# Values of the forgetting attention in one wide projection, and the memory's value columns moved one head pair earlier

## The chip, the cores and the metric

The kernel runs on one core of a Trainium2 chip. The core has a matrix engine (TensorE, PE in the rows; its weight loads are listed apart as PEld), a vector engine (VectorE, DVE), an activation engine (ScalarE, ACT), a general engine (GpSimd, POOL) and a queue that issues transfers (SyncE, SP). They run side by side, each through its own list of instructions in order, and wait for each other through semaphores. The metric is the time of one execution on the device in microseconds (us); the median of the runs counts.

## The reference

One layer of a hybrid encoder, 512 frames, width 1024. Cut to what matters here:

```python
hn = rmsnorm(h, norm_mix_g)
fq, fk, fv, ff, gq, gf, gi, gg = split(hn @ w_in)        # fq, fk, fv: 8 heads of 64
fox_out = fox_attention(fq, fk, fv, log_sigmoid(ff + b)) # causal, blocks of 128 queries
rec = hgrn2_chunkwise(gq, gf, gi, lbs) ...               # gated linear recurrence, 4 heads of 128
h = h + concat(fox_out, rec) @ w_out
mem_n = rmsnorm(mem, norm_mem_g)                         # 256 memory rows
k, v = split(mem_n @ w_xkv)                              # 1024 columns each
h = h + softmax((rmsnorm(h) @ w_xq) k / 16) v @ w_xo     # 4 heads of 256
h = h + square(relu(rmsnorm(h) @ w1)) @ w2
return rmsnorm(h, final_norm_g)
```

All inputs and results are float32, and every large product is made of three matmuls of a split type: each operand is kept as a rounded part (hi) and a remainder (lo), and hi*hi, hi*lo and lo*hi are added up.

## The kernel before

**Weights.** A list (`specs`, from line 126) names the weight panels in the order of their use. `next_panel` (line 214) keeps the panels loaded one ahead: a panel arrives as two units of 128x1024 elements, each of which ACT rounds to the hi part (`wh...`, line 171) and DVE subtracts to get the lo part (`wl...`, line 175). There are four buffers for hi and four for lo, so a unit can be split only when the PE has read the unit four places earlier. In the names, wh10b is the second unit of panel 10.

**Two ways to project.** `proj_tm` takes a panel of 256 columns: for every block of 128 frames, and every one of 8 slices of the width, three matmuls of 256 columns (lines 249 to 251). `proj_wide` and `gemm_wide` take 512 columns as two panels of four slices each: matmuls of 512 columns (lines 264 to 266) into four PSUM banks at once.

**Fill.** The order of the PE's instructions is that of the code (the other engines are ordered by a scheduler). The serial parts, the recurrence over four chunks and then the forgetting attention, are interleaved with a queue of independent projections: `fill.run(us)` takes steps from the queue until their nominal time reaches a credit, and `fill.until(name)` takes them until the projection of that name is done.

**Forgetting attention.** Four pairs of heads, for each four query blocks and two heads: 32 units. Per unit, in this order: the bias (POOL, `bi`), the scores (PE, `ps`, two matmuls with the keys `kh` and `kl`), a `fill.run(2.2)`, the product with the values of the unit three places before (PE, `pv`), and the transpose of the previous unit's probabilities (PE, `pt`). Between scores and transpose DVE takes the maximum (line 936), ACT the exponential (line 938), DVE normalises (line 940), and the transposed tile is copied out of PSUM (`pts`). A pair's queries and keys come from `fox_proj(p)` in the queue: 24 matmuls for the queries (`pq`) and 24 for the keys (`pk`); then DVE scales the keys (`ks`, line 759), ACT writes the rounded keys in four pieces (`kh`, lines 762 and 763, two pieces for each head) and DVE the remainders (`kl`, line 764). Before the first unit of pair p the code calls `fill.until("proj"+p)`.

**What the queue holds.** The values (`fv`) are projected in two panels of 256 columns: the first (for pairs 0 and 1) ahead of unit 2, the second in the steps of pair 1, finished by `fill.until("fv256")` before pair 2. The memory's rows are transposed (`mnt`) between the steps of `fox_proj(1)`; then follow the memory's value columns, 0 to 255 (`xv0`) in pair 0, the middle 512 (`xvw`) and the last 256 (`xv3`) in pair 2, and its four key panels (`xk`). What is left in the queue after the last unit is run before the next projection (`wo`).

Of the kernel before, what the change touches and what calls it, by code (L numbers as in the profile page):

```python
# [12 lines left out]
AF = mybir.ActivationFunctionType  # L13
# [4 lines left out]
S = 512  # L18
NT = S // P
# [3 lines left out]
WT = 256  # L23
FH = 8
FD = 64
# [6 lines left out]
GF = 5  # L32
WARM, WARM2 = 7, 4
P1, P2, P3, P4, PW = 20, 20, 20, 10, -20
MT, NF, V0, LAG = 3, 2, 1, 3
F1, F2, F3, F4, B1 = 1.6, 2.7, 1.5, 1.0, 2.0
A1, A2 = 1.4, 0.8
X1, X2, X3, X4 = 1.5, 2.0, 1.5, 2.0
# [4 lines left out]
def emit(  # L43
# [24 lines left out]
    x, mem, w_in, w_out = x[0], mem[0], w_in[0], w_out[0]  # L68
# [24 lines left out]
    def s4(shape, name, dt=F32):  # L93
        return s4p.tile([P] + shape, dt, tag="s4", name=name)
# [18 lines left out]
    def mm(name, shape=(S,)):  # L113
        return mmp.tile([P] + list(shape), F32, tag="mm", name=name)

    def pvt(name):
        return pvp.tile([P, S], F32, tag="pv", name=name)
# [11 lines left out]
    def panel(w, n0):  # L129
        return [(slice(0, WT), w[:, n0 : n0 + WT].rearrange("(k p) n -> p k n", p=P))]  # L130

    def wide(w, n0):

        return [[(slice(0, S), w[k0 * P : (k0 + 4) * P, n0 : n0 + S].rearrange("(k p) n -> p k n", p=P))] for k0 in (0, 4)]

    specs = []
# [4 lines left out]
    def pair(p):  # L141
        return [
            (slice(0, P), w_in[:, p * P : (p + 1) * P].rearrange("(k p) n -> p k n", p=P)),
            (slice(P, 2 * P), w_in[:, 512 + p * P : 512 + (p + 1) * P].rearrange("(k p) n -> p k n", p=P)),
        ]

    xv = [panel(w_xkv, D), *wide(w_xkv, D + WT), panel(w_xkv, D + 3 * WT)]
    specs += [pair(0), panel(w_in, 1024), pair(1), *xv[0:V0], pair(2), panel(w_in, 1024 + WT), pair(3), *xv[V0:]]
    for j in range(4):
        specs.append(panel(w_xkv, j * WT))  # L150
    for w in (w_out, w_xq, w_xo):
# [60 lines left out]
    def next_panel():  # L212
        while len(stream) < min(state["used"] + 2, len(specs)):
            for split in load_next():
                with ahead(PW):
                    split()
        r = stream[state["used"]]
        state["used"] += 1
        return r
# [95 lines left out]
    fill = Fill()  # L315
# [140 lines left out]
    with tc.manual_schedule(engines={mybir.EngineType.Activation, mybir.EngineType.DVE}):  # L456
# [94 lines left out]
        def qt_(h):  # L551
            return (Mv, Sa)[h % 2][h // 2][:, h % 2, :]
# [27 lines left out]
    for hp in range(2):  # L580
        wt = next_panel()
        for j in range(2):
            h = 2 * hp + j
# [6 lines left out]
    def proj_tm(dst, n0, func, name):  # L590
        wt = next_panel()
        for tp in range(2):
            ps = mm(f"{name}{n0}{tp}", (2, WT))
            for j in range(2):
                yield from gemm_tm(ps[:, j, :], wt, hn_hi, hn_lo, 2 * tp + j)
            for j in range(2):
                tb = 2 * tp + j
                ac.activation(dst(tb, n0), ps[:, j, :], func, scale=r0[:, tb : tb + 1])
# [4 lines left out]
    def proj_wide(dst, func, name):  # L603
        pss = [mm(f"{name}{tb}") for tb in range(NT - 1)] + [pvt(f"{name}3")]

        def done(tb, ps):
            ac.activation(dst[tb // 2][:, tb % 2, :], ps, func, scale=r0[:, tb : tb + 1])

        yield from gemm_wide(pss, hn_hi, hn_lo, done)
# [3 lines left out]
    fvt = []  # L613
# [25 lines left out]
    for hp in range(2):  # L639
# [8 lines left out]
        for j in range(2):  # L648
            h = 2 * hp + j
# [38 lines left out]
    for li, m in enumerate(mlev):  # L688
# [21 lines left out]
        for hp, ps in enumerate(lvs):  # L710
# [18 lines left out]
            for j in range(2):  # L729
                h = 2 * hp + j  # L730
                qv, kv, fv = halves(qt_(h), m), halves(kt_(h), m), halves(F_[:, j, :], m)
# [3 lines left out]
            fv = halves(F_.rearrange("p h t -> p (h t)"), m)  # L735
# [39 lines left out]
        fill.run(F4)  # L775


    def new_fv():
        t = s4([NT, WT], f"fv{len(fvt)}")
        fvt.append(t)  # L780
        return lambda tb, n0: t[:, tb, :]

    fill.add(proj_tm(new_fv(), 0, AF.Identity, "fv"), "fv0")
    fF = {}

    def fox_rows(p):
# [6 lines left out]
    def load_mem(t):  # L793
        m_ = s4([D], f"mt{t}")
        gp.dma_start(m_, mem[t * P : (t + 1) * P, :])
        norm_rows(m_, f"m{t}")
        mt.append(m_)

    load_mem(0)


    mx_hi, mx_lo = act_tile("mx_hi"), act_tile("mx_lo")
# [21 lines left out]
    for c in range(NT):  # L824
        cs = slice(c * P, (c + 1) * P)
        it = iv[c // 2][:, c % 2, :].rearrange("p (h v) -> p h v", v=P)
        gt = gg[c // 2][:, c % 2, :].rearrange("p (h v) -> p h v", v=P)
        po = sc(f"po{c}", (4, P))
        for h in range(4):
            te.matmul(po[:, h, :], Ag[h // 2][:, (h % 2) * 4 + c, :], it[:, h, :], start=True, stop=c == 0)  # L830
            if c > 0:
                te.matmul(po[:, h, :], qt_(h)[:, cs], St[:, h, :], start=False, stop=True)
        if c < NT - 1:
            pst = sc(f"pst{c}", (4, P))
            for h in range(4):
                te.matmul(pst[:, h, :], kts[c][:, h, :], it[:, h, :], start=True, stop=True)
            if c < NT - 2:
                k_T(c + 1)
            with ahead(P2):
                Sn = t2(f"S{c}", F32, (4, P))  # L840
                if c == 0:
                    ve.tensor_copy(Sn, pst)
                else:
                    for h in range(4):
                        ve.scalar_tensor_tensor(
                            Sn[:, h, :], St[:, h, :], Fg[h // 2][:, h % 2, c * P : c * P + 1], pst[:, h, :], op0=ALU.mult, op1=ALU.add
                        )
                St = Sn
        with ahead(P1):
            hs = sm(4, f"hs{c}")  # L850
            for h in range(4):
                j = t2(f"hj{c}{h}", F32, (P,))
                ac.activation(j, po[:, h, :], AF.Square, scale=128.0 ** -0.5, accum_out=hs[:, h : h + 1])
            hr = rstd_of(hs, 4, f"hr{c}")
            rec = t2(f"rec{c}", F32, (4, P))
            for h in range(4):
                ve.scalar_tensor_tensor(rec[:, h, :], po[:, h, :], hr[:, h : h + 1], gt[:, h, :], op0=ALU.mult, op1=ALU.mult)
        fill.run(H1)
        if c == MT:
            load_mem(1)  # L860
        if c == NF:
            fox_rows(0)
        if pending is not None:
            to_mix(*pending)
        pending = (c, rec)
        fill.run(H2)
# [11 lines left out]
    def mem_v_wide():  # L878
        js = slice(WT, 3 * WT)

        def done(t, ps):
            ac.activation(xvh[t][:, js], ps, AF.Copy)
            ve.tensor_tensor(xvl[t][:, js], ps, f(xvh[t][:, js]), ALU.subtract)

        yield from gemm_wide([mm(f"xvw{t}") for t in range(2)], me_hi, me_lo, done)
# [70 lines left out]
    def fox_out(p, tb):  # L956
        if tb == 0:
            fpv[p] = pvt(f"pv{p}")
        pv = fpv[p]
        ts_ = slice(tb * P, (tb + 1) * P)  # L960
        for sb in range(tb + 1):
            for j in range(2):
                h = 2 * p + j
                te.matmul(
                    pv[64 * j : 64 * j + 64, ts_],
                    fvt[h // 4][:, sb, h % 4 * FD : (h % 4 + 1) * FD],
                    probT[p, tb, j][:, sb * P : (sb + 1) * P],
                    start=sb == 0,
                    stop=sb == tb,
                )  # L970
        if tb == NT - 1:
            ac.activation(mx_hi[:, p, :], pv, AF.Copy)
            ve.tensor_tensor(mx_lo[:, p, :], pv, f(mx_hi[:, p, :]), ALU.subtract)
# [6 lines left out]
    for n in range(len(units) + LAG):  # L980
        if n < len(units):
            p, tb, j = units[n]
            if (tb, j) == (0, 0):
                fill.until(f"proj{p}")
                if p == 0:
                    fill.add(zipped(fox_proj(1), mem_T(), ZL), "proj1")
                    for i in range(V0):
                        fill.add(mem_v(i))
                elif p == 1:
                    fill.add(fox_proj(2), "proj2")  # L990
                    fill.add(proj_tm(new_fv(), WT, AF.Identity, "fv"), "fv256")
                elif p == 2:
                    fill.until("fv256")
                    fill.add(fox_proj(3), "proj3")
                    fill.add(mem_v_wide())
                    fill.add(mem_v(3))
                    for i in range(4):
                        fill.add(mem_k(i))
            if (tb, j) == (3, 0) and p < 3:
                fox_rows(p + 1)  # L1000
            if n == 2:
                fill.until("fv0")
            if n + 1 < len(units):
                fox_bias(units[n + 1])
            fox_scores(units[n])
        fill.run(A1 + A2)
        if n >= LAG and units[n - LAG][2] == 1:
            fox_out(*units[n - LAG][0:2])
        if 1 <= n <= len(units):
            fox_T(units[n - 1])  # L1010
# [461 lines left out]
```

## Time and profile before

| | |
|---|---|
| runs of the kernel before | 775.0, 775.82, 775.9 us; median 775.82 us |
| profiled execution | 775.59 us |
| span in the profile, first to last instruction | 773.9 us |
| outside the span (start and end) | 775.59 - 773.9 = 1.69 us |
| PE busy | 762.2 us, 98% of the span |
| DVE, ACT, POOL busy | 68%, 47%, 25% |
| granted TensorE clock | 0.998, the 2.4 GHz level |

A row of the time line gives the start in us from the start of the span, the duration, the engine, the line of the code, the operation, what is written and read by the program's names, and sizes; in brackets, how long the engine was idle before it and who ended that. Matmuls are pipelined, so a matmul's duration is longer than the distance to the next one: it is the distance between starts that adds up to the time.

### The profile page before, as it was taken

The numbers are of one execution on the slowest core, as the hardware profiler recorded it, in microseconds if no ns is written. First come the engines' busy times: TensorE is split into PE (matmuls) and PEld (weight loads), VectorE is DVE, ScalarE is ACT, GpSimd is POOL, SyncE is SP. The second block draws the span as 40 slices with busy tenths as digits, with TensorE's granted clock in tenths as the row PEclk, the third lists the DMA queues.
The fourth block names the chain that finished last, engine by engine and source line by source line (L and its number), as shares of the span: only waits on it lengthen the run. The fifth ranks groups of instructions, "written<-read, shape, count | busy, mean of one in ns | idle before, by whom it ended". The sixth has DMA issues, their size and how long they took to land.

```text
span 773.9 us, 11217 instructions
## 1 busy us (share of the span) xinstructions
PE 762.2 (98%) x4217; PEld 643.7 (83%) x4217; DVE 526.5 (68%) x847; ACT 367.0 (47%) x616; POOL 195.0 (25%) x263
## 2 busy tenths in 40 slices
PE   9999999999999999999999999999999999999995
PEld 6889889988879988888888788888888888888884
DVE  5647755587587656555548656959586867777795
ACT  5655465776465533244434245435353535343552
POOL 7207431434253025410016510100101010101123
PEclk9999999999999999999999999999999999999999
DMA  7553221233443343222113595565748475758502
GB/s 245 191 139 111 84 81 55 83 110 90 157 146 128 130 148 102 83 85 81 55 55 105 205 263 118 153 167 166 184 146 202 141 181 147 191 140 233 117 1 108
DMA packets 79832, 103.03 MB, mean 133 GB/s; under 512 B 4594, under 2 KB 58395, under 8 KB 79779
## 3 DMA queue, kind: packets, MB, share of 16 engines
q1 hardware_dynamic: 70226, 76.61, 31.1%
q0 software_dynamic: 8960, 24.67, 14.9%
q10 hardware_dynamic: 592, 1.05, 0.4%
q8 instruction: 33, 0.54, 0.3%
q14 instruction: 21, 0.16, 0.1%
HBM read 89.71 MB, written 4.21 MB: 121 GB/s over the span
## 4 chain that ended last, share of the span: by engine, by line
PE 98%; DVE 1%; issue 0%; POOL 0%; POOLq 0%; ACT 0%; DVEq 0%; ACTq 0%
PE u L236 8%; PE u L238 7%; PE u L237 7%; PE U L1352 4%; PE U L1354 4%; PE U L1353 4%; PE xq L236 2%; PE xq L237 2%; PE xw L238 2%; PE xq L238 2%; PE xw L236 2%; PE wo L236 2%; PE wo L237 2%; PE xw L237 2%; PE wo L238 2%; PE Y L1354 2%
## 5 line engine op out<-in xcount | busy, mean ns | idle before, releaser
L175 DVE TENSOR_TENSOR wld<-wq,whd 128x1024 fp32r<-128x1024 f32 x56 | 68.8, 1229 | 25.0 <-ACT whd L171 24.9
L236 PE MATMUL u<-x_hi,whu 128*128 128x512 f32 x192 | 74.7, 389 | 0.0
L237 PE MATMUL u<-x_lo,whu 128*128 128x512 f32 x192 | 74.7, 389 | 0.0
L238 PE MATMUL u<-x_hi,wlu 128*128 128x512 f32 x192 | 74.7, 389 | 0.0
L171 ACT ACTIVATE whd<-wq 128x1024 fp32r<-128x1024 f32 x56 | 58.4, 1052 | 30.5 <-PE u L237 21.6
L171 ACT ACTIVATE whu<-wru 128x1024 fp32r<-128x1024 f32 x24 | 25.3, 1053 | 60.7 <-DMA wru<-in_w_dram 60.7
L1226 POOL DMA_DIRECT2D wq<-in_w_dram x16 | 19.5, 1234 | 133.2 <-DMA wq<-in_w_dram 133.2
L175 DVE TENSOR_TENSOR wlu<-wru,whu 128x1024 fp32r<-128x1024 f32 x24 | 29.4, 1227 | 31.4 <-ACT whu L171 31.4
L1352 PE MATMUL U<-whd,hb 128*128 128x512 f32 x128 | 49.8, 389 | 0.0
L1353 PE MATMUL U<-wld,hb 128*128 128x512 f32 x128 | 49.8, 389 | 0.0
L1354 PE MATMUL U<-whd,hb 128*128 128x512 f32 x128 | 49.8, 389 | 0.0
L1226 POOL DMA_DIRECT2D wq<-wq x16 | 14.1, 879 | 123.3 <-DVE wld L175 96.3
L238 PEld LDWEIGHTS u<-x_hi,wlu 128*128 128x128 f32 x192 | 36.0, 188 | 7.5
L237 PEld LDWEIGHTS u<-x_lo,whu 128*128 128x128 f32 x192 | 36.0, 188 | 7.5
L236 PEld LDWEIGHTS u<-x_hi,whu 128*128 128x128 f32 x192 | 36.0, 188 | 7.4
L921 POOL TENSOR_SCALAR bi<-nF,Ft 128x128 f32<-128x128 f32 (+3 forms) x32 | 22.5, 702 | 42.3 <-PE pt L948 20.1
L1292 ACT ACTIVATE sq<-ur 128x512 f32<-128x512 f32 x32 | 20.0, 625 | 27.5 <-DVE ur L1289 27.5
L1289 DVE SCALAR_TENSOR_TENSOR ur<-u,rbc 128x512 f32<-128x512 f32 x32 | 21.9, 688 | 13.4 <-PE u L238 13.4
L938 ACT ACTIVATE bi<-bi,mx 128x128 f32<-128x128 f32 (+3 forms) x32 | 17.9, 560 | 23.3 <-DVE mx L936 23.1
L1353 PEld LDWEIGHTS U<-wld,hb 128*128 128x128 f32 x128 | 24.0, 188 | 5.0
L1354 PEld LDWEIGHTS U<-whd,hb 128*128 128x128 f32 x128 | 24.0, 188 | 5.0
L1352 PEld LDWEIGHTS U<-whd,hb 128*128 128x128 f32 x128 | 24.0, 188 | 5.0
(945 smaller groups left out, 2351.0 us busy)
## 6 DMA issues: line engine op xcount, KB each, us to landing
wq<-in_w_dram SPq DMA_DIRECT2D x40, 512.0 KB, 3.4
wru<-in_w_dram SPq DMA_DIRECT2D x24, 512.0 KB, 3.8
wq<-in_w_dram POOLq DMA_DIRECT2D x16, 512.0 KB, 8.2
wq<-wq POOLq DMA_DIRECT2D x16, 512.0 KB, 4.6
xTd<-xT POOLq DMA_DIRECT2D x4, 512.0 KB, 3.3
nF<-Fd POOLq DMA_DIRECT2D x8, 256.0 KB, 4.2
hT<-xTd POOLq DMA_DIRECT2D x4, 512.0 KB, 4.1
xt<-in_x_dram SPq DMA_DIRECT2D x3, 512.0 KB
```

The source lines that it names most:

```text
L171: ac.activation(hi, raw, AF.Copy)
L175: ve.tensor_tensor(lo, raw, f(hi), ALU.subtract)
L236: te.matmul(ps, wh, hi, start=n_ == 0 and not begun, stop=False)
L237: te.matmul(ps, wh, lo, start=False, stop=False)
L238: te.matmul(ps, wl, hi, start=False, stop=k == order[-1])
L921: gp.tensor_scalar(bi[:, 0:n], fF[h][:, 0:n], -1.0, Ft[:, tb, h : h + 1], op0=ALU.mult, op1=ALU.add)
L1226: gp.dma_start(raw.rearrange("p (k n) -> p k n", k=2), src, accum_op=ALU.add)
L1289: ve.scalar_tensor_tensor(u, ps, 0.0, rbc2, op0=ALU.max, op1=ALU.mult)
L1292: ac.activation(sqs[g, j][:, i, :], u, AF.Square)
L1352: te.matmul(ps, hi, whi[:, k, :], start=begin, stop=False, skip_group_check=True)
L1353: te.matmul(ps, hi, wlo[:, k, :], start=False, stop=False, skip_group_check=True)
L1354: te.matmul(ps, lo, whi[:, k, :], start=False, stop=k == 1, skip_group_check=True)
```

## The change

The two `proj_tm` projections of the values become one `proj_wide` over all 512 columns, whose end is awaited ahead of unit 2. The wide projection of the memory's middle value columns takes the place that the second half of the values had in the steps of pair 1; the last value columns and the key panels stay in pair 2. Values are stored by frame blocks instead of by head halves. The order of the weight panels follows. Both loads of the memory rows stand later in the code, inside the loop over the chunks.

```diff
-MT, NF, V0, LAG = 3, 2, 1, 3
+MT, NF, V0, LAG = 2, 2, 1, 3
...
-    specs += [pair(0), panel(w_in, 1024), pair(1), *xv[0:V0], pair(2), panel(w_in, 1024 + WT), pair(3), *xv[V0:]]
+    specs += [pair(0), *wide(w_in, 1024), pair(1), *xv[0:V0], pair(2), *xv[V0:3], pair(3), xv[3]]
...
-    def new_fv():
-        t = s4([NT, WT], f"fv{len(fvt)}")
-        fvt.append(t)
-        return lambda tb, n0: t[:, tb, :]
-
-    fill.add(proj_tm(new_fv(), 0, AF.Identity, "fv"), "fv0")
+    fvt.extend(s4([2, S], f"fv{t}") for t in range(2))
+    fill.add(proj_wide(fvt, AF.Identity, "fv"), "fv")
...
-    load_mem(0)
...
-        if c == MT:
-            load_mem(1)
+        if c >= MT:
+            load_mem(c - MT)
...
-                    fvt[h // 4][:, sb, h % 4 * FD : (h % 4 + 1) * FD],
+                    fvt[sb // 2][:, sb % 2, h * FD : (h + 1) * FD],
...
                     fill.add(fox_proj(2), "proj2")
-                    fill.add(proj_tm(new_fv(), WT, AF.Identity, "fv"), "fv256")
+                    fill.add(mem_v_wide())
                 elif p == 2:
-                    fill.until("fv256")
                     fill.add(fox_proj(3), "proj3")
-                    fill.add(mem_v_wide())
                     fill.add(mem_v(3))
...
             if n == 2:
-                fill.until("fv0")
+                fill.until("fv")
```

On the PE, from the last key matmul of pair 1 (`pk1`) to that pair's first scores (`ps20`, head 2, query block 0). Before:

```order
L238 MATMUL pk1_1862<-hn_hi_190,wl10b_1563 128x512
L385 MATMUL mnt7_1961<-ident_107,mt0_1361 128x128
L385 MATMUL mnt7_1961<-ident_107,mt1_1640 128x128
L249 MATMUL xv0_1992<-wh11a_1757,meh0_1778 128x256
...
L948 MATMUL pt02_2002<-ident_107,bi02_1870 128x128 x3
L930 MATMUL ps03_2017<-kh0_1432,q00_1327 128x512
...
L948 MATMUL pt12_2051<-ident_107,bi12_1903 128x128 x3
L930 MATMUL ps13_2062<-kh0_1432,q01_1328 128x512
...
L948 MATMUL pt03_2093<-ident_107,bi03_1944 128x128 x4
L930 MATMUL ps20_2106<-kh1_1858,q10_1769 128x128
L931 MATMUL ps20_2106<-kl1_1859,q10_1769 128x128
```

And with the change:

```order
L926 MATMUL ps13_2012<-kl0_1421,q01_1328 128x512
L236 MATMUL pk1_1914<-hn_hi_190,wh11b_1711 128x512
L237 MATMUL pk1_1914<-hn_lo_191,wh11b_1711 128x512
L238 MATMUL pk1_1914<-hn_hi_190,wl11b_1712 128x512
L385 MATMUL mnt7_2024<-ident_107,mt0_1564 128x128
L385 MATMUL mnt7_2024<-ident_107,mt1_1627 128x128
L249 MATMUL xv0_2055<-wh12a_1804,meh0_1825 128x256
...
L943 MATMUL pt03_2068<-ident_107,bi03_1926 128x128 x4
L925 MATMUL ps20_2080<-kh1_1910,q10_1816 128x128
L926 MATMUL ps20_2080<-kl1_1911,q10_1816 128x128
```

Where before the scores and products of two more units (head 0 and 1, query block 3) and 48 matmuls of `xv0` stood between, there now stand two transposes of `mnt`, 12 matmuls of `xv0` and four transposes.

The same on ACT, with the change, between the splits of panel 13 and the first probabilities of pair 1 (`bi_1964` is head 1, block 3; `bi_2007` head 2, block 0):

```order
L171 ACTIVATE wh13b<-wr13b 128x1024
L933 ACTIVATE bi_1964,dn_2017<-bi_1964,mx_2015 128x512
L387 ACTIVATE meh_1826<-mnt_2024,gv 128x256
L762 ACTIVATE kh_1910<-ks_2029 64x512
L763 ACTIVATE kh_1910<-ks_2029 64x512
L762 ACTIVATE kh_1910<-ks_2029 64x512
L763 ACTIVATE kh_1910<-ks_2029 64x512
```

A split, an exponential, a piece of the memory and the keys stand in a row there, as they did before for wh12b, with an exponential of 384 instead of 512 columns.

On the PE, from the last key matmul of pair 3 to that pair's first scores (`ps60`), with the change:

```order
L926 MATMUL ps53_2698<-kl2_2267,q21_2169 128x512
L236 MATMUL pk3_2637<-hn_hi_190,wh16b_2437 128x512
L237 MATMUL pk3_2637<-hn_lo_191,wh16b_2437 128x512
L238 MATMUL pk3_2637<-hn_hi_190,wl16b_2438 128x512
L249 MATMUL xv3_2730<-wh17a_2519,meh0_1825 128x256
L250 MATMUL xv3_2730<-wl17a_2520,meh0_1825 128x256
...
L943 MATMUL pt43_2743<-ident_107,bi43_2613 128x128 x4
L925 MATMUL ps60_2755<-kh3_2633,q30_2531 128x128
L926 MATMUL ps60_2755<-kl3_2634,q30_2531 128x128
```

Between them stand 12 matmuls of `xv3` and four transposes; before it was 36 wide matmuls of `xvw` and the scores, products and transposes of three units.

## Rows read from the trace of the kernel before

**Rows 1.** Page, part 1: busy time and share of each engine.
```profile
PE 762.2 (98%) x4217; PEld 643.7 (83%) x4217; DVE 526.5 (68%) x847; ACT 367.0 (47%) x616; POOL 195.0 (25%) x263
```

**Rows 2.** Waits of the PE, whole span: total us, times, longest.
```profile
PE warm L356 <- DVE ones L360: 1.3, 1, 1.3
PE pm L1068 <- DVE acc L1156: 1.0, 1, 1.0
PE lv L708 <- issue: 0.6, 1, 0.6
PE mnt L385 <- ACT pts L952: 0.2, 1, 0.2
```

**Rows 3.** Time line, PE, narrow value matmuls: first and last of 33.
```profile
141.56 0.28 PE L249 MATMUL fv<-wh9a,hn_hi 128*128 128x256 f32 x1
...
145.39 0.28 PE L251 MATMUL fv<-wh9b,hn_lo 128*128 128x256 f32 x1
```

**Rows 4.** Time line, PE, wide gate matmuls: first and last of 21.
```profile
89.43 0.39 PE L264 MATMUL gg<-wh6a,hn_hi 128*128 128x512 f32 x1
...
93.97 0.39 PE L266 MATMUL gg<-wh6b,hn_lo 128*128 128x512 f32 x1
```

**Rows 5.** Time line, PE, keys of pair 1 to its first scores.
```profile
165.36 0.39 PE L238 MATMUL pk<-hn_hi,wl10b 128*128 128x512 f32 x1
165.59 0.38 PE L385 MATMUL mnt<-ident,mt 128*128 128x128 f32 x2
165.72 0.37 PE L249 MATMUL xv<-wh11a,meh 128*128 128x256 f32 x1
165.93 0.28 PE L250 MATMUL xv<-wl11a,meh 128*128 128x256 f32 x1
...
173.85 0.60 PE L948 MATMUL pt<-ident,bi 128*128 128x128 f32 x4
174.20 0.31 PE L930 MATMUL ps<-kh,q 128*128 128x128 f32 x1
174.34 0.27 PE L931 MATMUL ps<-kl,q 128*128 128x128 f32 x1
```

**Rows 6.** Time line, ACT, same place.
```profile
165.55 1.06 ACT L171 ACTIVATE wh12b<-wr12b 128x1024 fp32r<-128x1024 f32 x1 [1.77 <-PE pk L237]
166.52 0.60 ACT L938 ACTIVATE bi<-bi,mx 128x384 f32<-128x384 f32 x1
167.03 0.18 ACT L938 ACTIVATION_READ_ACCUMULATOR bi<-bi,mx 128x1 f32 x1
167.12 0.45 ACT L387 ACTIVATE meh<-mnt,gv 128x256 fp32r<-128x256 f32 x1
167.47 0.62 ACT L762 ACTIVATE kh<-ks 64x512 fp32r<-64x512 f32 x1
168.12 0.63 ACT L763 ACTIVATE kh<-ks 64x512 fp32r<-64x512 f32 x1
```

**Rows 7.** Time line, DVE, same place.
```profile
165.79 0.69 DVE L759 TENSOR_TENSOR ks<-pk,rbc 128x512 f32<-128x512 f32 x1
166.65 1.23 DVE L175 TENSOR_TENSOR wl12b<-wr12b,wh12b 128x1024 fp32r<-128x1024 f32 x1 [0.17 <-ACT wh12b L171]
168.25 0.41 DVE L940 TENSOR_SCALAR bi<-bi,dn 128x384 f32<-128x384 f32 x1
168.57 0.68 DVE L764 TENSOR_TENSOR kl<-ks,kh 64x512 fp32r<-64x512 f32 x1
```

**Rows 8.** Groups by form, 120 to 290 us: exponential (120 to 210) and normalisation, 512 columns.
```profile
L938 ACT ACTIVATE bi<-bi,mx 128x512 f32<-128x512 f32 x4 | 2.9, 719 | 3.3 <-DVE mx L936 3.3
L940 DVE TENSOR_SCALAR bi<-bi,dn 128x512 f32<-128x512 f32 x8 | 4.1, 511 | 0.2
```

**Rows 9.** Time line, PE, keys of pair 3 to its first scores.
```profile
220.00 0.40 PE L238 MATMUL pk<-hn_hi,wl14b 128*128 128x512 f32 x1
220.23 0.39 PE L264 MATMUL xvw<-wh15a,meh 128*128 128x512 f32 x1
...
232.22 0.31 PE L930 MATMUL ps<-kh,q 128*128 128x128 f32 x1
```

## The prediction, made before the change was run

> **What bounds the kernel now.** I read the page's busy times first. The PE is busy for 762.2 of 773.9 us, no other engine for more than 68% [rows 1]. The second view is the PE's waits: four in all, 3.1 us together, and between 110 and 290 us, where the change works, one of 0.2 us, for a transpose of the memory [rows 2]. The third is the time line of the PE, for distances between starts. 33 narrow value matmuls follow each other in 3.83 us, 32 distances of 119.7 ns [rows 3]; 21 wide ones of the gate, which the same generator makes, in 4.54 us, 20 distances of 227.0 ns [rows 4]. So the PE's own list is the time in this stretch. An edit counts by the PE time that it removes, and by every wait that it brings into a list that has almost none. DVE, ACT, POOL and transfers count only where they end such a wait.
>
> **The removed matmuls.** Before, the values take 2 panels x 4 blocks x 8 slices x 3 = 192 narrow matmuls; now 96 wide ones. Each pair of narrow ones costs 239.4 ns, a wide one 227.0 [rows 3, 4]: 12.4 ns less, times 96 is 1.19 us. All of it is on the PE and nothing covers it, so it is a full gain. The starts are read to 0.01 us, 0.3 ns of a narrow distance and 0.5 ns of a wide one, so the bounds are 1.1 to 1.3; the pieces between which the projection is interleaved stay about as many.
>
> What is fixed in a matmul can also be had from the Trainium skill, "TensorE: Matmul & The Clock Gate", section "Back-to-back issue gap": at the full clock the distance is the columns over 2.4 GHz and 2.5 ns. By that rule two narrow ones cost 2.5 ns more than a wide one, 96 times 0.24 us, and the sum below would be 778.0 instead of 777.0. The rows disagree with it here: 119.7 and 227.0 ns where it has 109.2 and 215.8.
>
> **Evictions.** Eight ACT copies of 256 columns become four of 512. ACT is idle half of the time; at nothing. The wide projection takes three general PSUM banks and the one of the attention's output; the first bank is free again three blocks (18 wide matmuls, 4.1 us by [rows 4]) before the next projection asks for one, against one copy of some 0.7 us and one split of 1.06 us ahead of it [rows 6]: nothing.
>
> **The memory's loads and weight panels.** Both loads keep their place in POOL's list, ahead of the recurrence; only the normalisation moves back, and its first user moves back too, behind ten more us of value matmuls (96 times 227.0 ns against 96 times 119.7, [rows 3, 4]). With that the 0.2 us wait for ACT at the first transposes of the memory [rows 2] should go, since more time lies ahead of them: between 0 and 0.2, I take 0.2. SP's panels are as many and as large, in another order; each half of the wide values frees its buffers after 24 matmuls rather than at its end, so panels come earlier, not later: nothing.
>
> **The end of the queue.** Before, 36 narrow matmuls of the memory's keys stood between the last product and the output projection; now none. What was behind this cover is pair 3's result, which `wo` needs as its last slice, 21 wide matmuls or 4.8 us after its start [rows 4], against two copies of 0.7 us (as `ks` in [rows 7]): nothing.
>
> **The cover that goes.** Unit 2 now waits in the code for all of the values, so units 2 to 7 start `fox_proj(1)` later, and it ends in the steps of unit 7, just ahead of pair 1's first scores. Before, 8.84 us lay between the last key matmul and these scores [rows 5]; pair 3 had 12.22 [rows 9]. In both places I walk the chain by before's rows, from the start of the last key matmul.
>
> Pair 1, the PE's side: two transposes at 0.23, the first `xv0` at 0.36, its second at 0.57, ten more distances of 0.12, and four transposes of 0.35 in all [rows 3, 5]: the scores could start at 2.24, their second matmul at 2.38. ACT's side has the order that before had at its pair 1: the split waits for the PE's `pk` and starts at 0.19, then the exponential, a piece of the memory, the keys; the second piece ends at 168.75, that is 3.39 later [rows 6]. The exponential has now 512 columns, 0.12 more [rows 6, 8]: 3.51, and 0.04 of semaphore (the key's scaling starts 0.04 after the matmul's end, [rows 5, 7]). The scores wait 1.31 us. DVE's side: the remainder ends at 169.25, 3.89 later [rows 7], 0.10 to 0.12 more for the longer normalisation or exponential [rows 7, 8], in all 4.04: the second scores matmul brings the wait to 1.66.
>
> Pair 3: the first `xv3` follows at 0.23, twelve at 0.12 and four transposes of 0.35 give 2.02. On ACT the split starts at 0.19, the exponential at 1.16, the keys 0.72 after it, and two pieces take 1.28 [rows 6, 8]: 3.16 and 0.04. The wait is 1.18. The remainder ends at 3.22 and the second matmul stands at 3.34, so it adds nothing.
>
> Together 2.84 us. The bounds: with no split and no exponential ahead the keys would end at 0.43 + 0.69 + 1.28 + 0.04 = 2.44 [rows 5 to 7], the waits be 0.2 and 0.4, together 0.6; with one more split of 1.06 ahead in each place they would be 5.0. I take 2.84, because before's own rows are this very sequence. Behind the waiting scores stands the PE's whole list, so a wait is lost in full; nothing can be taken out of its turn.
>
> **The sum**, against the profiled execution's 775.59 us (span 773.9 and 1.69 outside): 775.59 - 1.19 - 0.2 + 2.84 = 777.04, 1.45 us or 0.19% more. That execution lies 0.23 under the median of the runs, 775.82. What a measurement of this kernel can tell from no change is 0.2%, 1.55 us; the forecast lies just inside.
>
> **Rivals.** First, slower than that line: ACT reaches the split late. Both places lie right behind scores of 512 columns, whose exponential comes in the same moment; before, ACT had been idle for 1.77 us at the split [rows 6], and that speaks against. If it is late by the exponential and a piece of the memory (0.72 and 0.45), or by another split, about 1.06 at one place, the time is 778.1; from 0.1 us of lateness on it decides. Second, the keys come earlier: the split waits longer for its buffer or panel than the exponential, and ACT's order is less tight than before's rows. At the lower bound of 0.6 for both waits the time is 775.59 - 1.39 + 0.6 = 774.8. For it speaks only that a list is no time, and that DVE or ACT may be ahead there; against, that the split can't start before the PE has read the panel's buffer, that its row begins as soon as this is so [rows 6], and that the list has split and exponential ahead of the keys. Third, no waits at all, only the gain: 774.2, 0.18% under; it would need the keys before the four transposes are through, 1.2 us ahead of the walk, and nothing in the rows speaks for it. Fourth, the wide value matmuls save a fifth of what the gate's rows say, 0.24 us: 778.0; the gate's 21 rows from the same generator speak against it. That is what the skill's fixed cost above would make of it.
>
> **Chances.** The forecast, with waits of 2.2 to 3.2 us (776.4 to 777.4): 0.57, of which 0.07 lie over the line of 0.2%. ACT late: 0.33. Earlier keys: 0.06, inside the line. No waits: 0.03; its time lies so near the line that I count it as faster. A smaller saving: 0.01. So slower 0.07 + 0.33 + 0.01 = 0.41, faster 0.03, same 0.56. The range reaches from the earlier keys, 774.8, to ACT late at both places by a little more than half a split, 778.4.
>
> **What would show it.** In the waits of the PE: two new rows, scores waiting for `kh` of 1.3 and 1.2 us, and a part of 0.3 to 0.4 for `kl`, near 178 and 233 us; no wait at the values, the memory's transposes or `wo`. In the time line: wide value matmuls 227 ns apart. On ACT: split, exponential and keys without a gap ahead of the scores. I am wrong if the scores of pairs 1 and 3 start without idle time ahead, if the wide values run at 239 ns or at 216, or if a wait stands elsewhere, at the banks of the values or at a panel.

## The result, and the profile after

The changed kernel takes 778.04 us (median of 19 runs, 777.16 to 779.39) against 775.87 us before (19 runs, 775.0 to 777.88): a ratio of 1.0027, with a 95% interval of 1.002 to 1.0034. That is 0.27% slower, just beyond the line of 0.2%. The forecast was 777.0, just inside that line; 778.04 lies beyond the line, but inside the range of 774.8 to 778.4. One thing is needed to read these numbers: about three in ten executions of the kernel before, and 9 of 19 of the changed one, are some 1.7 us longer than the others, for a reason that experiments 6 and 7 show. Half of the changed kernel's shorter executions lie at 777.53 or less.

The profiled execution took 778.04 us too, with a span of 776.2. The page's busy line, answering to [rows 1]:

```profile
PE 762.5 (98%) x4121; PEld 639.1 (82%) x4121; DVE 525.9 (68%) x847; ACT 367.0 (47%) x612; POOL 195.4 (25%) x263
```

The waits of the PE (total us, times, longest), answering to [rows 2]:

```profile
PE ps L925 <- ACT kh L763: 2.0, 2, 1.1
PE warm L356 <- DVE ones L360: 1.3, 1, 1.3
PE pm L1061 <- DVE acc L1149: 1.0, 1, 1.0
PE lv L708 <- issue: 0.6, 1, 0.6
PE ps L926 <- DVE kl L764: 0.2, 1, 0.2
```

There are 96 matmuls fewer, the wait for the memory's transposes is gone, and two waits of the scores for `kh` and one for `kl` are new. Busy time didn't fall by 1.2 us, because it counts a matmul to its modelled end and says little about distances. The values, in the time line of the PE (start, duration, instruction), first and last of 24 that follow each other:

```profile
155.85 0.39 PE L264 MATMUL fv<-wh10b,hn_hi 128*128 128x512 f32 x1
...
161.07 0.39 PE L266 MATMUL fv<-wh10b,hn_lo 128*128 128x512 f32 x1
```

That is 23 distances of 227.0 ns, as the gate's were [rows 4]. Pair 1's keys and scores, PE, answering to [rows 5]:

```profile
178.35 0.39 PE L238 MATMUL pk<-hn_hi,wl11b 128*128 128x512 f32 x1
178.58 0.38 PE L385 MATMUL mnt<-ident,mt 128*128 128x128 f32 x2
178.72 0.36 PE L249 MATMUL xv<-wh12a,meh 128*128 128x256 f32 x1
...
180.23 0.60 PE L943 MATMUL pt<-ident,bi 128*128 128x128 f32 x4
181.90 0.33 PE L925 MATMUL ps<-kh,q 128*128 128x128 f32 x1 [1.06 <-ACT kh L763]
182.46 0.33 PE L926 MATMUL ps<-kl,q 128*128 128x128 f32 x1 [0.24 <-DVE kl L764]
```

The scores' first matmul starts 3.55 us after the last key matmul, the second 4.11 us after it; the walk had 3.55 and 4.04. ACT and DVE in the same place, answering to [rows 6, 7]:

```profile
178.55 1.06 ACT L171 ACTIVATE wh13b<-wr13b 128x1024 fp32r<-128x1024 f32 x1 [2.21 <-PE pk L237]
179.51 0.71 ACT L933 ACTIVATE bi<-bi,mx 128x512 f32<-128x512 f32 x1
...
180.22 0.45 ACT L387 ACTIVATE meh<-mnt,gv 128x256 fp32r<-128x256 f32 x1
180.57 0.62 ACT L762 ACTIVATE kh<-ks 64x512 fp32r<-64x512 f32 x1
181.22 0.63 ACT L763 ACTIVATE kh<-ks 64x512 fp32r<-64x512 f32 x1
```

```profile
179.64 1.23 DVE L175 TENSOR_TENSOR wl13b<-wr13b,wh13b 128x1024 fp32r<-128x1024 f32 x1 [0.16 <-ACT wh13b L171]
...
181.24 0.48 DVE L935 TENSOR_SCALAR bi<-bi,dn 128x512 f32<-128x512 f32 x1
181.63 1.58 DVE L764 TENSOR_TENSOR kl<-ks,kh 64x512 fp32r<-64x512 f32 x2
```

Split, exponential, a piece of the memory and keys stand on ACT without a gap, and the split starts 0.20 us after the last key matmul (0.19 in the walk): ACT had been idle for 2.21 us, so the first rival, ACT late at the split, didn't come. Pair 3, PE, answering to [rows 9]:

```profile
235.32 0.39 PE L238 MATMUL pk<-hn_hi,wl16b 128*128 128x512 f32 x1
235.54 0.28 PE L249 MATMUL xv<-wh17a,meh 128*128 128x256 f32 x1
...
238.50 0.33 PE L925 MATMUL ps<-kh,q 128*128 128x128 f32 x1 [0.93 <-ACT kh L763]
238.77 0.33 PE L926 MATMUL ps<-kl,q 128*128 128x128 f32 x1
```

3.18 us, where the walk had 3.20. The second scores matmul stands 0.27 us behind the first, not 0.14 as in [rows 5]: it waits too, for DVE's remainder, which ends at 238.71. The list has no bracket for this wait, because the first matmul's modelled end, 238.83, covers it. The remainder took 0.88 us, not 0.68 as in [rows 7]:

```profile
237.83 0.88 DVE L764 TENSOR_TENSOR kl<-ks,kh 64x512 fp32r<-64x512 f32 x1
```

One more place differs, the start of the output projection:

```profile
275.88 0.83 PE L959 MATMUL pv<-pts,fv 128*64 128x128 f32 x12
276.63 0.50 PE L236 MATMUL wo<-mx_hi,wh22b 128*128 128x512 f32 x1
276.97 0.40 PE L237 MATMUL wo<-mx_lo,wh22b 128*128 128x512 f32 x1
```

Behind the attention's products its first two matmuls are 0.34 us apart. Before, behind the memory's keys, they were 0.23 apart (274.48 and 274.71). But then the keys stood behind those products, and their first two were 0.22 us apart, where 0.12 is usual:

```profile
270.06 0.39 PE L236 MATMUL xk<-meh,wh21b 128*128 128x256 f32 x1
270.28 0.28 PE L237 MATMUL xk<-mel,wh21b 128*128 128x256 f32 x1
270.40 0.28 PE L238 MATMUL xk<-meh,wl21b 128*128 128x256 f32 x1
```

From the last product to the 21st matmul of `wo` it is 4.91 us after, and before 9.18, of which 36 key matmuls at 119.7 ns are 4.31: 4.87. So this place costs 0.04 us.

To say what the change is worth I subtract the starts of the same instruction in two time lines, at three places: `pr` of the recurrence at 130 us, ahead of which the PE's lists are the same; the first `wo`; and the end of the span. All are against the kernel before, in us, one profiled execution each.

| kernel | at 130 us | at `wo` | at the end | from 130 us to the end |
|---|---|---|---|---|
| after | +0.56 | +2.15 | +2.31 | +1.75 |
| after, second profile (again) | +0.54 | +2.15 | +2.29 | +1.75 |
| narrow | +0.05 | +2.75 | +2.89 | +2.84 |
| cover | +0.13 | -1.35 | +0.40 | +0.27 |
| memT | +0.55 | -0.49 | +1.26 | +0.71 |
| cover3 | +0.07 | +0.34 | +0.49 | +0.42 |
| wideonly | +0.23 | +4.29 | +4.27 | +4.04 |
| halfkey | +0.28 | +3.89 | +4.04 | +3.76 |
| coverwarm | -0.19 | -1.58 | -1.42 | -1.23 |
| beforewarm | +0.19 | +0.19 | +0.22 | +0.03 |
| afterwarm | +0.01 | +1.64 | +1.76 | +1.75 |
| narrowcover | -0.24 | -0.58 | -0.41 | -0.17 |
| coverwarm2 | -0.34 | -1.81 | -1.67 | -1.33 |

The first column is that of equal programs: -0.34 to +0.56 us come and go in the first 20 us, most of it in the first 7, whatever the kernel (afterwarm has +0.01). The PE's warm-up shows how, before and after:

```profile
5.63 1.03 PE L461 MATMUL warm<-zero 128*128 128x512 bf16 x4
5.64 1.75 PE L461 MATMUL warm<-zero 128*128 128x512 bf16 x4
```

The four start alike, but their starts are 0.43 us apart after and 0.22 before; in both profiles the warm-up's first matmuls, from 1.7 us on, are 0.43 us apart. A factor of two is that between the two levels of the clock, 1.2 and 2.4 GHz, so the offset fits a clock that rises earlier in one execution than in another. The granted clock doesn't show it (the windows list 1.00 there), so this is argued from the distances. The last column is the kernel's own: +1.75 in three profiles of the changed order. From `wo` to the end the changed order adds 0.15 us. Most of that is no cost: what the products cost the next matmuls lies ahead of `wo` in the kernel before, and behind it here. Four kernels have a stretch of halved clock in it, cover and memT behind `wo`, wideonly and halfkey ahead of it; experiments 6 and 7 are about that.

### The profile page after: what moved, and what is told of

It reads as the page before. It is cut to its first block, busy times and chain, and to the rows that moved or that the text cites. A ratio compares the mean times of both kernels' runs of the same rounds, so it can differ in the third digit from the quotient of the medians.

```text
span 776.2 us, 11016 instructions
## 1 busy us (share of the span) xinstructions
PE 762.5 (98%) x4121; PEld 639.1 (82%) x4121; DVE 525.9 (68%) x847; ACT 367.0 (47%) x612; POOL 195.4 (25%) x263
## 4 chain that ended last, share of the span: by engine, by line
PE 97%; DVE 1%; issue 1%; ACT 0%; POOL 0%; POOLq 0%; DVEq 0%; ACTq 0%
PE u L236 8%; PE u L238 7%; PE u L237 7%; PE U L1347 4%; PE U L1345 4%; PE U L1346 3%; PE xq L236 2%; PE wo L236 2%; PE xq L237 2%; PE xw L237 2%; PE xw L236 2%; PE wo L237 2%; PE xq L238 2%; PE xw L238 2%; PE wo L238 2%; PE Y L1347 2%
## 5 line engine op out<-in xcount | busy, mean ns | idle before, releaser
L1044 ACT ACTIVATE x_hi<-hT,gv 128x512 fp32r<-128x512 f32 x16 | 11.5, 717 | 30.6 <-DVE hT L1043 30.6
```

## The experiments

My theory was that the change is worth 1.4 us, and that two waits, at places without cover, cost 2.8. Its rivals were that the wide matmuls save less, and that ACT is late as a whole, so that a wait is only moved.

**1. The changed kernel again (again).** No edit.

> The changed kernel as it is, beside the others of this call. Theory (two waits for the keys, 2.84 us together, against 1.39 saved): about 1.45 to 2.2 us over before, a ratio of 1.002 to 1.003, and in the profile the scores of pair 1 start 3.5 us and their second matmul 4.1 us after the last key matmul's start, those of pair 3 3.2 us. Rival for a part of the excess (the +0.5 us that the profile after has in the first 7 us, where both programs are the same): if it comes with the kernel it stands in this profile too; if it belongs to the execution, this profile's first 7 us differ from the profile after.

778.5 us (777.3 to 779.13, 6 runs), ratio 1.0034 (1.0022 to 1.0045). The same waits, and the +0.5 us of the first 7 us once more; only the later profiles showed that it isn't the kernel's, so this run by itself would have misled.

**2. Narrow values in the same order (narrow).**

```diff
... (the weight panels follow)
-    fill.add(proj_wide(fvt, AF.Identity, "fv"), "fv")
+    fill.add(proj_tm(rows_of(fvt), 0, AF.Identity, "fv"), "fv")
+    fill.add(proj_tm(rows_of(fvt), WT, AF.Identity, "fv"), "fv")
```

> As the changed kernel, but the values projected as two panels of 256 columns, both still ahead of unit 2, so that the order behind them stays. Theory of the removed matmuls (12.4 ns for each of 96 pairs): 1.2 us slower than the changed kernel of this call, with the same waits for the keys (3.5 and 3.2 us from the last key matmul to the scores). Rival (a fixed cost of 2.5 ns a matmul): 0.24 us slower. Second rival (the wide panel in front of the attention is what costs, by its buffers or evictions): not slower, or faster.

778.64 us (5 runs), ratio 1.0039 (1.0024 to 1.0054). The runs alone can't part this from the changed kernel. The profile can: 2.84 us from 130 us to the end, against 1.75 with the wide ones, with the scores at 3.55 and 4.11 us as there. The wide matmuls are worth 1.09 us in this place, or 11.4 ns a pair, where I had 12.4. Experiment 8 does it without the waits.

**3. Cover at both places (cover).**

```diff
+            if (tb, j) == (0, 0) and p:
+                fill.run((1.5, 0, 1.3)[p - 1])
             if n == 2:
                 fill.until("fv")
```

> As the changed kernel, with 1.5 us of queued work taken ahead of pair 1's first scores and 1.3 us ahead of pair 3's: by the order 15 matmuls of 256 columns of the memory's values stand there, between the transposes and the scores, and no matmul is added or left out. Theory (the loss is the two places without cover): both waits go, 2.8 us faster than the changed kernel of this call, 1.0 to 1.5 us faster than before, and the scores follow the matmul ahead of them within 0.3 us. Rival (the list of ACT is late as a whole, and the wait is only moved): waits of 1 us or more turn up at the next uses, and the gain is under 1 us.

775.96 us (774.15 to 776.79, 11 runs), ratio 0.9995 (0.9985 to 1.0006). The PE's waits in this profile:

```profile
PE warm L356 <- DVE ones L360: 1.3, 1, 1.3
PE pm L1063 <- DVE acc L1151: 1.0, 1, 1.0
PE lv L708 <- issue: 0.6, 1, 0.6
```

No wait is left between 110 and 290 us, and none turned up elsewhere. At `wo` this kernel is 1.48 us ahead of the kernel before (-1.35 less the +0.13 at 130 us), where the changed kernel was 1.59 behind: cover at two places is worth 3.07 us there. The scores follow at once, as the time line of the PE shows:

```profile
181.93 0.28 PE L251 MATMUL xv<-wh12a,mel 128*128 128x256 f32 x1
182.05 0.22 PE L925 MATMUL ps<-kh,q 128*128 128x128 f32 x1
182.11 0.28 PE L926 MATMUL ps<-kl,q 128*128 128x128 f32 x1
182.23 0.33 PE L249 MATMUL xv<-wh12a,meh 128*128 128x256 f32 x1
```

**4. The same by another edit (memT).** The memory's transposes are interleaved with the values, so that `fox_proj(1)` ends earlier.

```diff
-    fill.add(proj_wide(fvt, AF.Identity, "fv"), "fv")
+    fill.add(zipped(proj_wide(fvt, AF.Identity, "fv"), mem_T(), 20), "fv")
...
-                    fill.add(zipped(fox_proj(1), mem_T(), ZL), "proj1")
+                    fill.add(fox_proj(1), "proj1")
```

> As the changed kernel, but the memory's transposes are interleaved with the values instead of with pair 1's projection, so that this projection ends about 2 us of queue earlier. Theory: with the keys' last matmul a unit ahead of the scores in both pairs, both waits go: 2.5 to 2.8 us faster than the changed kernel of this call, 0.7 to 1.4 us faster than before. Rival (the memory's transposes wait for ACT's copies or for the load when they stand earlier): a wait at the memory's transposes of 0.5 us or more takes part of it back.

775.61 us (774.69 to 777.65, 11 runs), ratio 1.0001 (0.999 to 1.0013). Both waits for the keys are gone here too, a wait of 0.2 us at the memory's transposes is back, now for `mel`, and at `wo` it is 1.04 us ahead of the kernel before: less than cover, as the rival had it, but only in part.

**5. Cover at pair 3 alone (cover3).** The edit of cover with (0, 0, 1.5).

> As the changed kernel, with 1.5 us of queued work taken ahead of pair 3's first scores alone; pair 1 keeps its place. Theory (two separate waits, of 1.66 at pair 1 and 1.18 at pair 3): the wait of pair 3 goes and that of pair 1 stays as it was (3.5 and 4.1 us from the last key matmul to the two scores matmuls), 1.2 us faster than the changed kernel, about 0.5 us over before in executions without a stretch of halved clock. Rival (one late list of ACT that both share): the wait at pair 1 changes too, or pair 3's comes back at a later place.

776.29 us (775.81 to 778.15, 10 runs), ratio 1.0007 (0.9997 to 1.0018). Pair 1 keeps its wait (1.1 and 0.2 us in the waits of the PE, the scores 3.55 and 4.11 us after the last key matmul), pair 3 has none. From 130 us to the end 0.42 instead of 1.75: pair 3's place costs 1.33 us, and what is left to coverwarm's -1.23 or -1.33, 1.65 to 1.75 us, is pair 1's. The two waits are separate, and they have the sizes of the walk (1.18 and 1.66) and 0.15 or less each on top.

**6. The first half of the change alone, and a shorter ACT (wideonly, halfkey).** wideonly puts the middle of the memory's values back behind `fox_proj(3)`:

```diff
... (the weight panels follow)
                     fill.add(fox_proj(2), "proj2")
-                    fill.add(mem_v_wide())
                 elif p == 2:
                     fill.add(fox_proj(3), "proj3")
+                    fill.add(mem_v_wide())
```

> The first half of the change alone: the values wide and in front of the attention, but the middle of the memory's values back behind pair 3's projection. Theory: pair 1's wait of 1.66 stays; pair 3 has its cover again as in before, but the queue that fills the steps of pair 1 is short by 48 wide matmuls, or 10.9 us, less what until() pulls forward, and runs dry in its last steps, where a wait for the keys of pair 2 or for a transpose of the probabilities of 1 to 3 us turns up near 200 to 205 us; by the replay of the order at before's durations it is 1.2 us slower than the changed kernel. Rival (the second half is what costs): pair 3's wait goes and nothing new comes, 1.2 us faster than the changed kernel.

780.1 us (4 runs), ratio 1.0058 (1.0044 to 1.0071). Pair 3's wait is gone and the queue runs dry at the end of pair 1, as expected, with one new wait in the time line of the PE:

```profile
204.83 0.40 PE L926 MATMUL ps<-kl,q 128*128 128x512 f32 x1
207.03 0.63 PE L943 MATMUL pt<-ident,bi 128*128 128x128 f32 x4 [1.80 <-DVE bi L935]
```

So the second half of the change, the queue's, makes good what the first half would cost. It is 2.1 us slower than the changed kernel, though, not 1.2. Behind that wait the PE runs at half its clock for a while; stretches of 2 us (busy time of PE, PEld, DVE, ACT and POOL, then the granted clock, DMA share, GB/s):

```profile
204.00:206.00 2.00, 1.23 (x11) 0.62 (x7) 1.86 (x4) 1.98 (x5) 0.80 (x2) 1.00 0.61 222
206.00:208.00 2.00, 0.97 (x7) 0.95 (x8) 2.00 (x6) 1.93 (x5) 1.85 (x5) 0.96 0.46 142
208.00:210.00 2.00, 2.00 (x6) 1.54 (x6) 1.60 (x6) 1.29 (x3) 1.53 (x3) 0.50 0.35 129
210.00:212.00 2.00, 2.00 (x8) 1.55 (x6) 0.45 (x2) 0.26 (x2) 0.00 (x0) 0.69 0.00 0
```

1.2 instead of 2.4 GHz there; the share of the clock that is missing, 2 us times 0.04, 0.50 and 0.31, is 1.7 us.

halfkey has POOL copy one of the two pieces of keys that the scores waited for:

```diff
-            ac.activation(kh[r2, j, :], t[r, :], AF.Copy)
+            if j:
+                ac.activation(kh[r2, j, :], t[r, :], AF.Copy)
+            else:
+                gp.tensor_copy(kh[r2, j, :], t[r, :])
```

> As the changed kernel, but the second half of the first head's keys (one of ACT's two copies ahead of the scores) is copied by POOL. Theory (two chains end together, ACT's with kh and DVE's with the remainder kl): the first scores matmul waits up to 0.6 us less in each place, the second then waits for kl instead, and the sum of both waits falls by 0.2 us at most. Rival (ACT's copies alone are the wait): 0.6 us less in each place, 1.2 us faster than the changed kernel.

779.57 us (778.01 to 779.98, 4 runs), ratio 1.0045 (1.0028 to 1.0062). Neither had it right. Pair 1 in the time line of the PE:

```profile
177.80 0.39 PE L238 MATMUL pk<-hn_hi,wl11b 128*128 128x512 f32 x1
...
180.78 0.30 PE L928 MATMUL ps<-kh,q 128*128 128x128 f32 x1 [0.50 <-POOL kl L755]
182.36 0.33 PE L929 MATMUL ps<-kl,q 128*128 128x128 f32 x1 [1.28 <-DVE kl L767]
```

The first scores matmul comes 0.57 us earlier, 2.98 us after the key matmul, as half of ACT's copies are gone; the second comes 0.45 us later, at 4.56. So ACT's copies are not the whole wait, DVE's remainder stands behind them. Why it came later stands on DVE:

```profile
179.09 1.66 DVE L175 TENSOR_TENSOR wl13b<-wr13b,wh13b 128x1024 fp32r<-128x1024 f32 x1 [0.16 <-ACT wh13b L171]
```

Beside POOL's copy of 0.61 us the split takes 1.66 us instead of 1.23. It does so in three of the four splits that lie beside such a copy (1.66 to 1.68 us). There the copy had started first, by 0.02 to 0.03 us; at 134.87 us the split had, by 0.22 us, and took 1.22 us, while that copy took 2.06. Of the other splits between 120 and 290 us all but three stay under 1.25. The Trainium skill, "GPSIMD Engine Reference", section "1. Specifications", has POOL and VectorE on shared SBUF interfaces, with contention for DVE instructions that read two SBUF inputs; the split reads two, and the rows agree. A halved stretch follows pair 1's wait here as well: the granted clock is 0.91, 0.50 and 0.73 in the three windows of 2 us from 182 us on, which is 1.7 us again.

**7. The stretch of halved clock (coverwarm, beforewarm, afterwarm).** In the profiles of cover and memT the PE loses time behind the wait for the norm ahead of the MLP, near 441 us, which the expectations call the last norm. Windows of cover:

```profile
440.00:442.00 2.00, 1.02 (x10) 0.86 (x8) 1.07 (x4) 0.82 (x4) 1.43 (x2) 1.00 1.05 390
442.00:444.00 2.00, 2.00 (x9) 1.64 (x9) 0.16 (x1) 0.00 (x0) 1.84 (x3) 0.79 1.05 374
444.00:446.00 2.00, 2.00 (x7) 1.54 (x6) 0.00 (x0) 0.00 (x0) 0.50 (x1) 0.50 1.11 344
446.00:448.00 2.00, 2.00 (x9) 1.66 (x8) 0.64 (x1) 1.06 (x1) 0.00 (x0) 0.86 1.10 255
```

The profiles before and after have the same wait of 1.0 us [rows 2] and a clock of 1.00 there. So it comes in some executions and not in others. The edit gives the PE four matmuls whose result nobody reads, in the time in which it waits:

```diff
+    hold = pvt("hold")
+    for _ in range(4):
+        te.matmul(hold, x2_hi[:, 0, 0:P], x2_hi[:, 0, :], start=True, stop=True)
     ms2 = mean_sq(ssq2, "pm2")
```

> As the kernel with cover at both places (label cover), and four matmuls of 512 columns whose result nobody reads in the 0.98 us in which the PE waits ahead of the last norm's one-column matmuls, near 441 us. In the profiles of cover and memT the granted clock is halved for 3 to 4 us right behind this place, and eight matmuls take 0.43 us instead of 0.23 there; the profiles after and again lack this. Theory (this stretch is what sets the longer executions of every kernel here apart): no execution has it any more, all lie near the shorter ones of cover, 774.1 to 774.6, and the ratio to before is 0.997 to 0.998. Rival (the halved stretch comes by itself, whatever the PE does ahead of it): as many long executions as cover has, 776.3 to 776.8, half of them. Second rival (the four matmuls delay the norm): all executions 0.3 us or more over 774.5.

774.65 us, 774.26 to 775.21 in all 11 runs, ratio 0.9984 (0.9976 to 0.9993): no long execution is left. The granted clock stays at 1.00 there, and the norm's matmuls follow the four without a wait:

```profile
439.71 1.17 PE L1417 MATMUL hold<-x_hi 128*128 128x512 f32 x4
440.94 1.02 PE L1063 MATMUL pm<-ones,ssq 128*128 128x1 f32 x8
```

> The kernel of the label coverwarm once more, beside beforewarm on one chip. Theory: 774.3 to 775.2 again, 0.9 to 1.3 us under beforewarm (the saved 1.1 and 0.2 us, less up to 0.2 at the output projection's first matmuls), a ratio to before of 0.998 with an interval under 1. Rival (the first time was a lucky chip): ratio 0.9995 to 1.0005.

774.6 us (774.0 to 775.2, 11 runs), ratio 0.9977 (0.9969 to 0.9986), the same again. It is 1.09 us under the next kernel, beforewarm, as expected.

> The kernel before, with the four unread matmuls in the 0.98 us wait ahead of the last norm and nothing else. Theory (of the kernel before, only this place lets the clock fall): its longer executions, 777.1 to 777.9, a third of all, are gone, and all lie at 775.0 to 775.9, where its shorter ones lie. Rival (the fall comes by itself): a third of them still lies above 777.

775.69 us, 775.2 to 776.09 in all 12 runs, ratio 0.9993 (0.9985 to 1.0002), while 7 of the 35 runs of the kernel before lay above 777.

> The changed kernel with the same four matmuls. Theory one (its own two waits of 1.2 to 1.7 us let the clock fall as well): some executions stay 1.5 us or more above the others, with a halved stretch behind 182 or 239 us; the shorter ones are at 777.2 to 777.9. Theory two (only the last norm's wait does): no long executions, all at 777.2 to 778.0. By either theory the shorter ones are 1.8 to 2.1 us over those of beforewarm: 0.24 to 0.27%, the change by itself.

777.76 us, 777.08 to 778.38 in all 12 runs, ratio 1.0019 (1.001 to 1.0027). Theory two: in the changed order only the wait for that norm lets the clock fall, its own two waits didn't in 12 executions. Without that stretch in either, the change costs 777.76 less 775.69, 2.07 us.

**8. Narrow values without the waits (narrowcover).** The edits of narrow and of coverwarm together.

> As the kernel with cover at both places and the four unread matmuls (label coverwarm), but with the values projected as two panels of 256 columns. Theory: the wide matmuls alone are worth 1.1 to 1.2 us (12.4 ns a pair): 775.5 to 776.0, no wait at the keys. Rival (2.5 ns a matmul): 0.24 us over coverwarm, 774.8 to 774.9.

775.33 us (775.02 to 776.12, 11 runs), ratio 0.9991 (0.9982 to 1.0). That is 0.7 us over coverwarm, between the two expectations. In the profiles it is 1.06 and 1.16 us from 130 us to the end (-0.17 against -1.23 and -1.33). The difference lies outside the span: the time less the span is 1.82 us here in the mean of the runs and 2.03 with the wide ones. The matmuls themselves are worth 1.1 us.

## Why the prediction was nearly right

- **The removed matmuls**: 1.19 foretold, 1.06 to 1.16 in narrow and narrowcover. The distance of 227.0 ns holds in the 24 matmuls above, but inside all pieces of the values together the mean in the profile after is 228.0, which is 0.1 us over 96 matmuls. A piece's first matmul stands further from its second, which equal distances don't have: 0.29 us behind scores and 0.31 behind transposes. Narrow ones lose nearly as much (0.17 and 0.20 in narrow, where 0.12 is usual), so this changes the saving little. The fourth rival, 0.24 us, is out. The Trainium skill, "TensorE: Matmul & The Clock Gate", section "Back-to-back issue gap", would have it so by its fixed part of 2.5 ns, which it gives for a single matmul; the distances here and both pairs of profiles disagree with it.
- **The memory's transposes**: their wait is gone, as foretold.
- **Where the waits come, and from which chain**: right in place, engine and time to 0.07 us (3.55, 4.11 and 3.18 us against 3.55, 4.04 and 3.20), but for pair 3's second scores matmul (see the next point). Cover takes the waits away, at one place or at both. In pair 1's walk on the PE the "ten more distances" are eleven; its sum, 2.24, has eleven.
- **The size of the waits**: the mis-sized term, 2.84 foretold and 3.0 to 3.1 found. The walk gave DVE's remainder 0.68 us, from a row of before with no POOL work beside it; it took 0.78 at pair 1 and 0.88 at pair 3. At pair 3 it ended 3.39 us after the key matmul, not 3.22, so the step "it adds nothing" failed: the second scores matmul started at 3.45 instead of 3.34. Counted to the second scores matmul of each pair, which the PE's side allows at 2.38 and 2.16, the waits are 1.73 and 1.29, or 3.02 in all. POOL's bias (`bi`) runs beside both remainders. In all 14 profiles together, none of the 60 remainders without POOL work beside them took more than 0.69 us, and each that took 0.77 or more lay beside that bias. Others beside it took 0.69, so what in it slows DVE is not shown.
- **The end of the queue, "nothing"**: 0.04 us. What `wo` now loses behind the products, the keys lost before.
- **The sum**: 3.0 to 3.1 for the waits and 0.04 at the end of the queue, less 1.1 and 0.2, is 1.7 to 1.8; the time lines have 1.75. Foretold was 1.45.
- **What lies around the span**: I took it as the same, 1.69 us. In the means of the runs it is 1.71 before and 1.86 after. With the 1.75 that makes 1.9; the shorter executions' medians differ by 1.9 (777.53 against 775.67), afterwarm's and beforewarm's by 2.07.
- **The median** of the changed kernel lies 0.5 us over that of its shorter executions, as 9 of 19 were long. Whether it falls into the halved clock more often than the kernel before (6 of 19 in the same comparison) stays open.

So the slower side of 0.2% was reached not by a rival but by small terms of 0.1 to 0.2 us (the saving, the waits, what lies around the span), all on the same side of a forecast that stood 0.1 us from the line, and by the long executions in the median. I gave "slower" 0.41, and 0.33 of that to a mechanism, ACT late, that didn't happen. That 778.04 lies inside the range is in part luck: the forecast's own band ended at 777.4, and the room above it stood there for ACT late.

The version that beats both kernels is coverwarm: the change, its cover put back, and the four unread matmuls, 0.16 and 0.23% under the kernel before in two comparisons.

## What to carry to other kernels

When the PE's own list is the time, an edit that saves matmuls also moves every producer that was hidden behind them: list for each moved projection how much work lies between its last matmul and its first use, and put some of the queue there before counting the gain. A duration taken from a row holds for what ran beside it there: check what the other engines do at the new place. A chain of copies on two engines ends where the later one does, so shortening one of them may buy nothing. If a sum of small terms ends close to the line that decides, the chance belongs on both sides of it, even where the mechanism is sure.

## What the runs showed of the hardware

- A wait of 0.98 us and eight one-column matmuls were followed by a stretch at half the clock in some executions and not in others, at a price of 1.6 to 1.7 us; waits of 1.80 us (wideonly) and of 0.50 and 1.28 us (halfkey) were followed by one in the profiles taken. Waits of 1.06 and 0.24 us at pair 1 were not, in three profiles of the changed order (after, again, afterwarm). Four unread matmuls in the first of these waits removed the stretch in all 57 runs of the four kernels that have them (narrowcover among them): none lies over 1.4 us above the fastest of its kernel.
- A DVE subtraction of 128x1024 from two SBUF tiles took 1.66 us instead of 1.23 while POOL copied 64x512, in the three places of halfkey where the copy had started first. Where the subtraction had, it took 1.22 and the copy 2.06 instead of 0.61.
- A DVE subtraction of 64x512 took 0.66 to 0.69 us in all 60 cases without POOL work beside it, and up to 0.88 (after) and 1.15 (before) beside POOL's bias.
- The time outside the span differs between programs: 1.71 us before, 1.86 after and 2.03 for coverwarm in the means of their runs. Runs of one program can differ too, 1.72 to 1.98 in narrowcover. Why is open.
